# Strassen's scheme for the output products of the state-space part and of the last feed-forward

## Chip, cores, metric

The kernel runs on one core of a Trainium2 chip. The metric is the device time of one execution in microseconds (us); for the kernel before it is 3130.28 us, the median of three runs (3128.58 to 3131.64).

## What is computed

Two residual networks, one after the other, on 512 tokens of width 1024, all in float32. The first has a mixer of pooling and gated recurrence and a feed-forward part, then attention and a feed-forward part. The second, cut to what matters here, is

```python
for layer in range(DEPTH):                      # DEPTH = 2
    if layer < N_A_LAYERS:                      # layer 0: state space
        x = x + _mamba2_mixer(_rms_norm(x, a_norm[i]), ...)
    else:                                       # layer 1: attention with dilated windows
        ...
        x = x + _dilated_mixer(_rms_norm(x, b_norm[j]), k_sh, v_sh, ...)
    x = x + _conv_ffn(_rms_norm(x, ffn_norm[layer]), ...)
return _rms_norm(x, final_norm)
```

`_mamba2_mixer` ends in `y @ w_out` with y of 512 x 2048 and w_out of 2048 x 1024. `_conv_ffn` ends in `(silu(gate) * val) @ w_down` with a left side of 512 x 2816 and w_down of 2816 x 1024. The change is about the first of these and about the `w_down` of layer 1, which is the last product of the kernel.

## The kernel before, in words

Every large product is made three times as precise as one pass of TensorE in its float32r format gives: each operand is split into a high part h (a ScalarE copy into float32r, L312 or L321) and the rest l (a VectorE subtraction, L314 or L322), and `mm3` (L327 to L331) adds three matmuls, h*h, h*l and l*h, into one PSUM bank. Weights come in pieces of 128 x 1024 floats (512 KB) through `load_w`: SyncE's DMA into the tile wr (3 buffers), ScalarE's wh and VectorE's wl (4 buffers each).

`out_phase` makes an output product. The left side G (Y in the state-space part, GF in the feed-forward part) lies with its contraction index over the partitions, as nk pieces of 128 x 512 tokens. For each half hf of the 1024 output columns it takes four banks, one for each tile t of 128 tokens, and goes through the nk pieces: a `Jit` object splits G[:, k] just then into jh and jl, and four `mm3` calls of 128x512 follow. For the last six pieces of the second half it goes by tiles, so that tile after tile is finished and can be used early. A finished bank is handed to `use`: `residual_add` (L1202) adds it to x on VectorE; in the last feed-forward part `final_use` (L1632) also squares, scales and stores it.

What runs beside it: in `mamba` eight groups of heads (`ssd_group`) each make four heads' outputs, whose end is a chain over VectorE, ScalarE, GpSimd and TensorE (y, its squares, gms, the transposes yt, Y at L1414). `out_phase` needs Y piece by piece, so its first products stand in TensorE's queue among those of the last group. After it, `fill` makes the next part's normalized input: x is scaled (xn, L355), transposed (tr) and split; an `anchor` among the last products sets from where on TensorE takes these transposes. The order on every queue is made by a scheduler when the program is built; `high_priority(60)` lets the weights' loads and splits go ahead. Tiles come from pools; a tile whose memory still has a user waits for that user alone.

Of the kernel before, what the change touches and what calls it, by code (L numbers as in the profile page):

```python
# [9 lines left out]
FT = mybir.dt.float32  # L10
FR = mybir.dt.float32r
# [3 lines left out]
AF = mybir.ActivationFunctionType  # L15
# [4 lines left out]
P = 128  # L20
# [3 lines left out]
SEQ = 512  # L24
CTX = 256
TOK = SEQ + CTX
HID = 22
# [9 lines left out]
class Params:  # L37
# [5 lines left out]
    def add(self, name, width):  # L43
        self.off[name] = (self.n, width)
        self.n += width
# [161 lines left out]
class Jit:  # L207
# [5 lines left out]
    def pair(self, n):  # L213
        return [self.pool.tile([P, n], FR, name="j" + x, tag="j" + x, bufs=self.bufs) for x in "hl"]
# [30 lines left out]
class Body:  # L245
# [157 lines left out]
    def fill(self, norm, more=()):  # L403

        xt = self.xt
        part = lambda a: self.to_channels(
            self.scr, [self.x[:, t] for t in (a, a + 1)], self.p(norm), None, *xt[0], a * P,
            [(self.p(nm), *xt[1 + i]) for i, nm in enumerate(more)])
        with self.tc.issue_after(self.anchor):
            part(0)  # L410
        self.leave(lambda: part(2))
# [129 lines left out]
    def out_phase(self, pair, wap, nk, tiles, use, tail=3, order=None, first=0):  # L541

        for hf in range(2):
            acc = {t: self.bank("acc") for t in tiles}
            k0s = list(range(first, nk, 2))
            cut = len(k0s) - tail if hf else len(k0s)
            for k0 in k0s[:cut]:
                wh, wl = self.load_w(wap[:, hf, k0:k0 + 2])  # L550
                for k in range(k0, k0 + 2):
                    gh, gl = pair(k)
                    for t in tiles:
                        s = slice(t * P, (t + 1) * P)
                        self.mm3(acc[t], gh[:, s], gl[:, s], wh[:, k - k0], wl[:, k - k0], k == first, k == nk - 1)
            if cut == len(k0s):
                for t in tiles:
                    use(hf, t, acc[t])
                continue
            w = [(k0, self.load_w(wap[:, hf, k0:k0 + 2])) for k0 in k0s[cut:]]  # L560
            ks = [k0 + i for k0 in k0s[cut:] for i in (0, 1)]
            g = {k: pair(k) for k in ks} if not hasattr(pair, "tile") else None
            for t in order or tiles:
                s = slice(t * P, (t + 1) * P)
                gt = pair.tile(ks, t) if g is None else None
                for k0, (wh, wl) in w:
                    for i in (0, 1):
                        k = k0 + i
                        gh, gl = (g[k][0][:, s], g[k][1][:, s]) if g else (gt[0][:, k - ks[0]], gt[1][:, k - ks[0]])
                        self.mm3(acc[t], gh, gl, wh[:, i], wl[:, i], k == first, k == nk - 1)  # L570
                        if k == ks[1]:

                            self.anchor = self.last_mm
                use(hf, t, acc[t])

    def residual_norm(self, pool, x_of, row_of, tiles):

        nc = self.nc
        st = {}

        def use(hf, t, b):
            row = row_of(t)
            y = pool.tile([P, 512], FT, name=f"y{hf}", tag=f"y{hf}", bufs=2 if hf else tiles)
            if hf == 0:
                ms = pool.tile([P, 3], FT, name="yms", tag="yms", bufs=6)
                st[t] = (y, ms)
            y0, ms = st[t]
            self.squares(pool, b, ms[:, hf:hf + 1])
            nc.vector.tensor_mul(y, b, row[:, hf * 512:(hf + 1) * 512])
            if hf == 0:  # L590
                return
            r = ms[:, 2:3]
            nc.gpsimd.tensor_add(r, ms[:, 0:1], ms[:, 1:2])
            self.rstd(r, 1)
            x = x_of(t)
            for i, src in ((0, y0), (1, y)):
                s = slice(i * 512, (i + 1) * 512)
                nc.vector.scalar_tensor_tensor(x[:, s], src, r, x[:, s], op0=OP.mult, op1=OP.add)

        return use  # L600
# [598 lines left out]
        self.split(QH[:, hs, q], QL[:, hs, q], ob.rearrange("p (h q) -> p h q", h=4))  # L1199


    def residual_add(self, hf, t, b):  # L1202
        x = self.x[:, t, hf * 512:(hf + 1) * 512]
        self.nc.vector.tensor_add(x, x, b)
# [13 lines left out]
    def mamba(self, alloc, fill):  # L1218
        nc = self.nc
        es = ExitStack()  # L1220
        yp = self.pool("ssmy", es=es)
        Y = yp.tile([P, 16, SEQ], FT, name="Y")
        with ExitStack() as es1:
# [22 lines left out]
            b = self.bank("dt")[:32]  # L1246
            for k in range(KT):
                self.mm3(b, dh[:, k], dl[:, k], XH[:, k], XL[:, k], k == 0, k == KT - 1)
            with ExitStack() as es2:
                tp = self.pool("soft2", es=es2)  # L1250
                t = lambda n: tp.tile([32, SEQ], FT, name=n)
                v, u, z, w, acc = t("spv"), t("spu"), t("spz"), t("spw"), t("spa")
# [14 lines left out]
                b = self.bank("dtt")  # L1267
# [7 lines left out]
            b = self.bank("cs")  # L1275
# [19 lines left out]
        self.prepare(alloc)  # L1295
        with ExitStack() as es2:
            op = self.pool("ssmo", es=es2)
            self.out_phase(Jit(self, op, Y, SEQ, 3), self.a["wm_out"], 16, range(4), self.residual_add)
        fill()
        es.close()  # L1300

# [114 lines left out]
    def conv_ffn(self, l, side, alloc=None, fill=None):  # L1416
        nc = self.nc
        es = ExitStack()
        (XH, XL), = self.xt
        GF = self.pool(f"ug{l}", es=es, side=side).tile([P, HID, SEQ], FT, name="GF")  # L1420
        es2 = ExitStack()
        op = self.pool(f"uo{l}", es=es2, side=side)
        taps = self.p(f"fcw{l}").rearrange("p (a b) -> p a b", b=3)
        st = {}
        with ExitStack() as es1:
            tp = self.pool(f"ut{l}", es=es1, side=side)

            def use(j, i, b):
                k, val = j // 2, j % 2
                t = tp.tile([P, SEQ], FT, name="cv", tag=f"cv{val}", bufs=2)  # L1430
                self.conv(t, b, taps[:, HID * val + k], 3)
                if not val:
                    nc.scalar.activation(t, t, AF.Silu)
                    st[0] = t
                else:
                    nc.vector.tensor_mul(GF[:, k], t, st[0])

            self.in_phase(XH, XL, self.a[f"u{l}_in"], range(2 * HID), ((0, SEQ),), use, 3, HALVES)
        self.nes.close()
        if alloc:  # L1440
            self.prepare(alloc)
        self.out_phase(Jit(self, op, GF, SEQ, 3), self.a[f"u{l}_out"], HID, range(4),
                       self.residual_add if alloc else self.final_use(es2, side))
        es2.close()
        if fill:
            fill()
        es.close()
# [252 lines left out]
```

## Time and profile before

| what | us |
|---|---|
| median of three runs | 3130.28 |
| the profiled execution, its own time | 3131.54 |
| its span, first to last instruction | 3129.8 |
| TensorE (PE) busy, 15850 matmuls | 3055.1 |
| VectorE (DVE) busy | 1903.4 |
| ScalarE (ACT) busy | 1294.4 |
| GpSimd (POOL) busy | 138.1 |

The profile is of one execution; 1.7 us of its time lie outside the span. Times of the trace count from the span's start. Matmul records overlap, since the engine is a pipeline: the distance from start to start tells what one costs. The brackets behind a row give the idle time before it and what ended it. The granted clock of TensorE is full in nearly all of the span (0.997 on average).

### The profile page before, as it was taken

Reading aid. Unit: us, or ns where it says so; the run is one execution under the profiler, and the core shown is the slowest. Engines: PE = TensorE matmul, PEld = TensorE weight load, DVE = VectorE, ACT = ScalarE, POOL = GpSimd, SP = SyncE. Lnnn points to the kernel's source line nnn. Section 1 sums busy time; section 2 is a strip of 40 time slices with the busy share of each in tenths; the row PEclk is TensorE's granted clock in tenths of the full one; section 3 lists DMA queues with packets and bytes.
Section 4 is the critical chain, followed back from the end, with each engine's and each line's share of the span. In section 5 each row is a group of like instructions: output and inputs, shape, how many; then the busy total and the mean of one; then the engine's idle time right before and its main releaser. Section 6 shows DMA issues by size and latency. Waiting matters only on the chain. (4 is left out here: it accounts for less than half of the span.)

```text
span 3129.8 us, 40785 instructions
## 1 busy us (share of the span) xinstructions
PE 3055.1 (98%) x15850; PEld 2567.9 (82%) x15850; DVE 1903.4 (61%) x3252; ACT 1294.4 (41%) x2354; POOL 138.1 (4%) x244
## 2 busy tenths in 40 slices
PE   7999999999998999999999999999999999999999
PEld 6888788888886777888888888788888987788887
DVE  7996677532346677233567777665555687765555
ACT  4333451111335666222455455443334444543334
POOL 1000010000003101000010000000000000000000
PEclk9999999999999999999999999999999999999999
DMA  6621236632221111333322222233333321123332
GB/s 228 186 80 41 95 111 205 204 118 64 74 68 43 55 48 53 103 95 101 95 64 81 68 81 68 81 95 95 97 99 88 104 81 55 54 85 98 95 106 76
DMA packets 80929, 292.31 MB, mean 93 GB/s; under 512 B 9744, under 2 KB 10432, under 8 KB 79840
## 3 DMA queue, kind: packets, MB, share of 16 engines
q1 hardware_dynamic: 79104, 285.48, 30.2%
q0 software_dynamic: 1056, 3.17, 0.3%
q8 instruction: 125, 2.05, 0.3%
q10 hardware_dynamic: 576, 1.05, 0.1%
q14 instruction: 68, 0.56, 0.1%
HBM read 287.54 MB, written 2.12 MB: 93 GB/s over the span
## 5 line engine op out<-in xcount | busy, mean ns | idle before, releaser
L314 DVE TENSOR_TENSOR wl<-wr,wh 128x1024 fp32r<-128x1024 f32 x420 | 513.3, 1224 | 460.2 <-ACT wh L312 456.3
L312 ACT ACTIVATE wh<-wr 128x1024 fp32r<-128x1024 f32 x424 | 447.8, 1057 | 769.6 <-PE in L330 530.4
L329 PE MATMUL acc<-wh,jh 128*128 128x512 f32 x1080 | 424.4, 393 | 7.1 <-ACT jh L321 4.9
L331 PE MATMUL acc<-wh,jl 128*128 128x512 f32 x1080 | 422.0, 393 | 3.4 <-DVE jl L322 3.4
L330 PE MATMUL acc<-wl,jh 128*128 128x512 f32 x1080 | 423.5, 392 | 0.0
L322 DVE TENSOR_TENSOR jl<-GF,jh 128x512 fp32r<-128x512 f32 (+1 forms) x170 | 132.5, 781 | 233.9 <-ACT jh L321 230.2
L329 PEld LDWEIGHTS acc<-wh,jh 128*128 128x128 f32 x1080 | 203.2, 188 | 50.6 <-ACT jh L321 6.6
L321 ACT ACTIVATE jh<-GF 128x512 fp32r<-128x512 f32 (+1 forms) x170 | 119.0, 701 | 300.4 <-PE acc L330 288.8
L330 PE MATMUL in<-xtf0L,wh 128*128 128x256 f32 (+1 forms) x728 | 241.9, 332 | 0.0
L329 PE MATMUL in<-xtf0H,wh 128*128 128x256 f32 (+1 forms) x728 | 241.6, 332 | 0.0
L331 PEld LDWEIGHTS acc<-wh,jl 128*128 128x128 f32 x1080 | 202.9, 188 | 46.8 <-DVE jl L322 5.9
L331 PE MATMUL in<-xtf0H,wl 128*128 128x256 f32 (+1 forms) x728 | 241.2, 331 | 0.0
L330 PEld LDWEIGHTS acc<-wl,jh 128*128 128x128 f32 x1080 | 203.3, 188 | 40.6
L452 DVE SCALAR_TENSOR_TENSOR junkv<-wr,srow 128x1024 bf16<-128x1024 f32 x128 | 156.5, 1222 | 66.3 <-DMA wr<-ada 63.8
L329 PEld LDWEIGHTS in<-xtf0H,wh 128*128 128x128 f32 x728 | 138.3, 190 | 13.6
L331 PEld LDWEIGHTS in<-xtf0H,wl 128*128 128x128 f32 x728 | 138.1, 190 | 13.2
L330 PEld LDWEIGHTS in<-xtf0L,wh 128*128 128x128 f32 x728 | 138.3, 190 | 12.7
L330 PE MATMUL in<-xtf10L,wh 128*128 128x512 f32 (+1 forms) x376 | 141.2, 377 | 0.7 <-DVE xtf10L L322 0.4
L330 PE MATMUL in<-xtv0L,wh 128*128 128x512 f32 (+1 forms) x376 | 141.3, 376 | 0.0
L331 PE MATMUL in<-xtv0H,wl 128*128 128x512 f32 (+1 forms) x376 | 141.3, 376 | 0.0
L331 PE MATMUL in<-xtu0H,wl 128*128 128x512 f32 (+1 forms) x376 | 141.3, 376 | 0.0
L330 PE MATMUL in<-xtu0L,wh 128*128 128x512 f32 (+1 forms) x376 | 141.2, 376 | 0.0
(449 smaller groups left out, 6673.9 us busy)
## 6 DMA issues: line engine op xcount, KB each, us to landing
wr<-f_in SPq DMA_DIRECT2D x88, 512.0 KB, 3.6
wr<-u_in SPq DMA_DIRECT2D x88, 512.0 KB, 3.6
wr<-ada SPq DMA_DIRECT2D x80, 512.0 KB, 4.4
wr<-f_out SPq DMA_DIRECT2D x44, 512.0 KB, 3.6
wr<-u_out SPq DMA_DIRECT2D x44, 512.0 KB, 3.6
wr<-w_in SPq DMA_DIRECT2D x32, 512.0 KB, 3.8
wr<-wm_x SPq DMA_DIRECT2D x32, 512.0 KB, 3.6
wr<-wd_q SPq DMA_DIRECT2D x24, 512.0 KB, 3.5
```

Of the source, the lines that this page charges most:

```text
L312: nc.scalar.activation(h, raw, AF.Copy)
L314: (engine or nc.vector).tensor_sub(l, raw, h.bitcast(FT))
L321: nc.scalar.activation(h, src, AF.Copy)
L322: nc.vector.tensor_sub(l, src, h.bitcast(FT))
L329: mm(out, wh, xh, start=first, stop=False)
L330: mm(out, wh, xl, start=False, stop=False)
L331: self.last_mm = mm(out, wl, xh, start=False, stop=last).ins
L452: nc.vector.scalar_tensor_tensor(self.junkv, raw, 1.0, self.srow[:, v], op0=OP.mult, op1=OP.mult, accum_out=self.mc[l, v][:, j:j + 1])
```

## The change

Both output products are made by a new method `seven`, with Strassen's scheme in the form of Winograd. The tokens are halved (t0 and t1, 256 each), the contraction index is halved (k and half + k) and the output columns are halved (the two 512-wide parts of wap). Of the eight half-size products seven are left, of sums of the blocks. A first loop over half = nk/2 pieces makes four of them (m1, m6, m5, m4, eight banks in all) and a second loop the other three (m2, m3, m7). The sums of G's blocks are VectorE's (one of them GpSimd's in the second loop), the sums of the weights' blocks are GpSimd's: three of 128x512 in each step of the first loop, one in each of the second. The results of the first loop are joined on ScalarE and VectorE (c1, c2, c3) and added to x by GpSimd in the second loop (`residual_part`), two of 128x512 in each of four steps. Each weight is loaded once in the first loop, and three of four blocks again in the second. The other feed-forward part and the other products stay as they are. The last feed-forward part's pool for all this is opened later than the one before.

```diff
...
+    def seven(self, pool, G, wap, nk, use, add):
...
+        def raw(src, own):
+            r = (pool if own else self.wp).tile([P, 2, 512], FT, name="wr", tag="wr", bufs=2 if own else 3)
+            nc.sync.dma_start(r if len(src.shape) == 3 else r[:, 0], src)
+            return r
+        def right(r):
+            h, l = [self.wp.tile([P, 2, 512], FR, name="w" + x, tag="w" + x, bufs=4) for x in "hl"]
+            self.split(h, l, r)
+            return h, l
+        def left():
+            return [pool.tile([P, 4, H], FR, name="s" + x, tag="s" + x, bufs=3) for x in "hl"]
+        def sums():
+            return pool.tile([P, 2, H], FT, name="ss", tag="ss", bufs=2)
+        def product(m, k, hl, i, wh, wl, ts=(0, 1)):
+            for t in ts:
+                s = slice(t * P, (t + 1) * P)
+                self.mm3(m[t], hl[0][:, i, s], hl[1][:, i, s], wh, wl, k == 0, k == half - 1)
+        m1, m6 = [[self.bank("acc") for _ in range(2)] for _ in range(2)]
+        m5, m4 = [[self.bank("m") for _ in range(2)] for _ in range(2)]
+        part = {}
+        for k in range(half):
+            with self.tc.high_priority(60):
+                a, b = raw(wap[:, :, k], False), raw(wap[:, :, half + k], True)
+                g.tensor_sub(a[:, 1], a[:, 1], a[:, 0])
+                g.tensor_sub(b[:, 1], b[:, 1], a[:, 1])
+                g.tensor_sub(b[:, 0], b[:, 1], b[:, 0])
+                (ah, al), (bh, bl) = right(a), right(b)
+            s, hl = sums(), left()
+            dve.tensor_add(s[:, 0], G[:, k, t1], G[:, half + k, t1])
+            dve.tensor_sub(s[:, 1], s[:, 0], G[:, k, t0])
...
+            self.split(hl[0][:, :2], hl[1][:, :2], ends)
+            self.split(hl[0][:, 2:], hl[1][:, 2:], s)
+            nc.scalar.activation(G[:, half + k, t1], s[:, 1], AF.Copy)
+            last = k == half - 1
+            product(m1, k, hl, 0, ah[:, 0], al[:, 0])
...
+            product(m6, k, hl, 3, bh[:, 1], bl[:, 1])
+            if last:
+                for i in range(2):
+                    part[0, 2 + i] = pool.tile([P, 512], FT, name=f"c3{i}")
+                    dve.tensor_add(part[0, 2 + i], m6[i], part[0, i])
+            product(m5, k, hl, 2, ah[:, 1], al[:, 1])
+            if last:
+                for i in range(2):
+                    part[1, i] = part[1, 2 + i] = pool.tile([P, 512], FT, name=f"c2{i}")
+                    dve.tensor_add(part[1, i], m5[i], part[0, 2 + i])
+            product(m4, k, hl, 1, bh[:, 0], bl[:, 0])
+            if last:
+                for i in range(2):
+                    dve.tensor_sub(part[0, 2 + i], part[0, 2 + i], m4[i])
+        m2, m3 = [[self.bank("acc") for _ in range(2)] for _ in range(2)]
+        m7 = [self.bank("m") for _ in range(2)]
+        kept = []
+        todo = [(hf, t) for t in range(4) for hf in range(2)]
+        for k in range(half):
+            with self.tc.high_priority(60):
+                b, a = raw(wap[:, :, half + k], True), raw(wap[:, 1, k], False)
+                g.tensor_sub(a[:, 0], b[:, 1], a[:, 0])
+                bh, bl = right(b)
+                th, tl = [pool.tile([P, 512], FR, name="t" + x, tag="t" + x, bufs=3) for x in "hl"]
+                self.split(th, tl, a[:, 0])
+            s, hl = sums(), left()
+            dve.tensor_sub(s[:, 0], G[:, half + k, t0], G[:, half + k, t1])
+            g.tensor_sub(s[:, 1], G[:, k, t0], G[:, k, t1])
+            self.split(hl[0][:, 0], hl[1][:, 0], G[:, half + k, t0])
+            self.split(hl[0][:, 1:3], hl[1][:, 1:3], s)
+            if k:
+                for hf, t in todo[:2]:
+                    add(hf, t, part[hf, t])
+                todo = todo[2:]
+            last = k == half - 1
+            for i in range(2):
+                product(m2, k, hl, 0, bh[:, 0], bl[:, 0], (i,))
+                product(m3, k, hl, 1, bh[:, 1], bl[:, 1], (i,))
+                if last:
+                    use(0, i, m2[i])
+                    use(1, i, m3[i])
+            if k < half - 2:
+                product(m7, k, hl, 2, th, tl)
+            else:
+                kept.append((k, hl, 2, th, tl))
+        for i in range(2):
+            for args in kept:
+                product(m7, *args, (i,))
+            if i == 0:
+                self.anchor = self.last_mm
+            for hf in range(2):
+                use(hf, 2 + i, m7[i])
...
+    def residual_part(self, hf, t, part):
+        x = self.x[:, t, hf * 512:(hf + 1) * 512]
+        self.nc.gpsimd.tensor_add(x, x, part)
...
         with ExitStack() as es2:
             op = self.pool("ssmo", es=es2)
-            self.out_phase(Jit(self, op, Y, SEQ, 3), self.a["wm_out"], 16, range(4), self.residual_add)
+            self.seven(op, Y, self.a["wm_out"], 16, self.residual_add, self.residual_part)
         fill()
         es.close()
@@ -1419,7 +1537,8 @@
         (XH, XL), = self.xt
         GF = self.pool(f"ug{l}", es=es, side=side).tile([P, HID, SEQ], FT, name="GF")
         es2 = ExitStack()
-        op = self.pool(f"uo{l}", es=es2, side=side)
+        if alloc:
+            op = self.pool(f"uo{l}", es=es2, side=side)
...
         self.nes.close()
         if alloc:
             self.prepare(alloc)
-        self.out_phase(Jit(self, op, GF, SEQ, 3), self.a[f"u{l}_out"], HID, range(4),
-                       self.residual_add if alloc else self.final_use(es2, side))
+            self.out_phase(Jit(self, op, GF, SEQ, 3), self.a[f"u{l}_out"], HID, range(4), self.residual_add)
+        else:
+            op = self.pool(f"uo{l}", es=es2, side=side)
+            self.seven(op, GF, self.a[f"u{l}_out"], HID, self.final_use(es2, side), self.residual_part)
         es2.close()
         if fill:
             fill()
```

On TensorE's queue at the end of the state-space part (yd, yo and yt belong to the last group of heads, the acc of L329 to L331 to the output product) stood before:

```order
L1399 MATMUL yo<-H,Cc 128x256
L331 MATMUL acc<-wh,jl 128x512
L329 MATMUL acc<-wh,jh 128x512
L330 MATMUL acc<-wl,jh 128x512
L331 MATMUL acc<-wh,jl 128x512
L1390 MATMUL yd<-xdt,M_16273 128x128 x3
L1390 MATMUL yd<-xdt,M_16243 128x128
L1390 MATMUL yd<-xdt,M_16253 128x128
L1390 MATMUL yd<-xdt,M_16263 128x128
L1390 MATMUL yd<-xdt,M_16273 128x128
L1399 MATMUL yo<-H,Cc 128x256
L329 MATMUL acc<-wh,jh 128x512
```

and now stands, up to the first products of the new method:

```order
L1517 MATMUL yo<-H,Cc 128x256
L1508 MATMUL yd<-xdt,M_16273 128x128 x3
L1508 MATMUL yd<-xdt,M_16243 128x128
L1508 MATMUL yd<-xdt,M_16253 128x128
L1508 MATMUL yd<-xdt,M_16263 128x128
L1508 MATMUL yd<-xdt,M_16273 128x128
L1517 MATMUL yo<-H,Cc 128x256
L1530 MATMUL yt<-ident,y 128x128 x8
L329 MATMUL acc<-wh,sh 128x512
L330 MATMUL acc<-wl,sh 128x512
```

Before, 61 matmuls of the output product stood ahead of the group's last transpose; now none does.

On GpSimd's queue there was nothing between the last group's gms and the ms of the next part:

```order
L342 TENSOR_SCALAR gms_15861<-gms_15861 128x4
L343 TENSOR_TENSOR gms_15861<-gms_15861,mhalf_77 128x4
L342 TENSOR_SCALAR gms_16275<-gms_16275 128x4
L343 TENSOR_TENSOR gms_16275<-gms_16275,mhalf_77 128x4
L342 TENSOR_SCALAR ms_16974<-ms_16974 128x1
```

In the first loop it now has, for one piece after another (the first tile of a pair of wr is a, the second b):

```order
L617 TENSOR_TENSOR wr_16514<-wr_16514,wr_16512 128x512
L618 TENSOR_TENSOR wr_16514<-wr_16514 128x512
L616 TENSOR_TENSOR wr_16610<-wr_16610 128x512
L617 TENSOR_TENSOR wr_16563<-wr_16563,wr_16561 128x512
L618 TENSOR_TENSOR wr_16563<-wr_16563 128x512
```

and VectorE in the same steps:

```order
L322 TENSOR_TENSOR wl_16569<-wr_16561,wh_16568 128x1024
L322 TENSOR_TENSOR sl_16627<-Y_12795,sh_16626 128x512
L322 TENSOR_TENSOR wl_16573<-wr_16563,wh_16572 128x1024
L322 TENSOR_TENSOR sl_16627<-ss_16625,sh_16626 128x512
L621 TENSOR_TENSOR ss_16723<-Y_12795 128x256
L622 TENSOR_TENSOR ss_16723<-ss_16723,Y_12795 128x256
```

The subtraction of a (L616) goes two pieces ahead of those of b (L617, L618), and VectorE's six operations of a step are two splits of weights, two of the left side and two sums.

## Rows read from the trace of the kernel before

**Rows 1.** The page, part 1: busy us (share of the span) and instructions.

```profile
PE 3055.1 (98%) x15850; PEld 2567.9 (82%) x15850; DVE 1903.4 (61%) x3252; ACT 1294.4 (41%) x2354; POOL 138.1 (4%) x244
```

**Rows 2.** Timeline of PE at the last product: start, us, what [idle before].

```profile
3117.66 0.39 PE L329 MATMUL acc<-wh,jh 128*128 128x512 f32 x1
...
3122.20 0.39 PE L331 MATMUL acc<-wh,jl 128*128 128x512 f32 x1
```

**Rows 3.** Timeline of POOL, then of DVE, 12 to 53 us.

```profile
12.80 2.35 POOL L314 TENSOR_TENSOR wl<-wr,wh 128x1024 fp32r<-128x1024 f32 x1
...
36.51 5.92 POOL L314 TENSOR_TENSOR wl<-wr,wh 128x1024 fp32r<-128x1024 f32 x2 [9.46 <-ACT wh L312]
45.47 2.98 POOL L314 TENSOR_TENSOR wl<-wr,wh 128x1024 fp32r<-128x1024 f32 x1 [3.04 <-ACT wh L312]
...
36.16 0.69 DVE L322 TENSOR_TENSOR XL<-mod,XH 128x512 fp32r<-128x512 f32 x1
36.77 3.43 DVE L671 SCALAR_TENSOR_TENSOR junkv<-wo,srow 128x1024 bf16<-128x1024 f32 x1
...
46.18 2.55 DVE L322 TENSOR_TENSOR XL<-mod,XH 128x256 fp32r<-128x256 f32 x1
...
51.55 0.41 DVE L322 TENSOR_TENSOR XL<-mod,XH 128x256 fp32r<-128x256 f32 x1
51.88 1.21 DVE L671 SCALAR_TENSOR_TENSOR junkv<-wo,srow 128x1024 bf16<-128x1024 f32 x1
```

**Rows 4.** Timeline of POOL, then of DVE, 991 to 997 us.

```profile
995.99 0.74 POOL L378 TENSOR_TENSOR x1L<-mod,x1H 128x256 fp32r<-128x256 f32 x1 [2.12 <-ACT x1H L377]
...
991.38 0.42 DVE L322 TENSOR_TENSOR x1L<-mod,x1H 128x256 fp32r<-128x256 f32 x1
...
996.25 0.75 DVE L322 TENSOR_TENSOR x1L<-mod,x1H 128x256 fp32r<-128x256 f32 x1 [0.69 <-ACT x1H L321]
```

**Rows 5.** Last group and first output products: timeline of DVE and ACT, group of PE.

```profile
1955.73 1.23 DVE L314 TENSOR_TENSOR wl<-wr,wh 128x1024 fp32r<-128x1024 f32 x1 [6.99 <-ACT wh L312]
1956.87 0.68 DVE L1344 TENSOR_TENSOR xdt<-xt,dtT 128x512 f32<-128x512 f32 x1
...
1972.64 0.69 DVE L1382 TENSOR_TENSOR M<-sg,cbm 128x512 f32<-128x512 f32 x1 [0.27 <-ACT sg L1380]
...
1978.97 0.69 DVE L322 TENSOR_TENSOR jl<-Y,jh 128x512 fp32r<-128x512 f32 x1
...
1985.30 1.27 ACT L1414 ACTIVATE Y<-yt,prm 128x512 f32<-128x512 f32 x2
...
L329 PE MATMUL acc<-wh,jh x28: 387/389/582, 1964.3 to 1989.8; 128*128 128x512 f32 x28
```

**Rows 6.** Groups by line, ACT: busy us, mean ns of one, idle before.

```profile
L312 ACT ACTIVATE wh<-wr 128x1024 fp32r<-128x1024 f32 x424 | 447.8, 1057 | 769.6 <-PE in L330 530.4 <-DMA wr<-f_in 115.0 <-PE acc L331 52.0
...
L321 ACT ACTIVATE jh<-GF 128x512 fp32r<-128x512 f32 (+1 forms) x170 | 119.0, 701 | 300.4 <-PE acc L330 288.8 <-DVE GF L1436 11.6
```

**Rows 7.** Stretches: length, busy us of PE, PEld, DVE, ACT, POOL, clock, DMA, GB/s.

```profile
2064.00:2068.00 4.00, 4.00 (x35) 4.00 (x34) 1.92 (x3) 1.15 (x2) 0.73 (x2) 1.00 0.97 362
```

**Rows 8.** End of the first output product: group of PE, timeline of DVE.

```profile
L331 PE MATMUL acc<-wh,jl x101: 389/389/477, 1990.2 to 2060.2; 128*128 128x512 f32 x101
...
2053.37 0.75 DVE L355 TENSOR_SCALAR xn<-x,ms 128x1024 f32<-128x1024 f32 x1 [2.19 <-POOL ms L343]
```

**Rows 9.** Timeline at the start of the last product: PE, DVE.

```profile
3002.55 0.39 PE L329 MATMUL acc<-wh,jh 128*128 128x512 f32 x1
...
3006.32 0.69 DVE L1436 TENSOR_TENSOR GF<-cv 128x512 f32<-128x512 f32 x1
```

**Rows 10.** Timeline of PE after a long wait.

```profile
48.78 0.79 PE L331 MATMUL acc<-wh,XL 128*128 128x512 f32 x1 [5.37 <-DVE XL L322]
49.38 0.63 PE L329 MATMUL acc<-wh,XH 128*128 128x512 f32 x1
49.80 0.63 PE L330 MATMUL acc<-wl,XH 128*128 128x512 f32 x1
```

More of the change, by code (lines that the diff above doesn't have):

```diff
@@ L574, in out_phase @@
                 use(hf, t, acc[t])
+    def seven(self, pool, G, wap, nk, use, add):
+        nc, half, H = self.nc, nk // 2, 2 * P
+        t0, t1 = slice(0, H), slice(H, 2 * H)
+        T = G.shape[2]
+        dve, g = nc.vector, nc.gpsimd
+        def raw(src, own):
[27 more added lines that the diff above has]
+            dve.tensor_sub(s[:, 1], s[:, 0], G[:, k, t0])
+            base = G[:, k, 0:1]
+            ends = bass.AP(tensor=base.tensor, offset=base.offset,
+                           ap=[list(base.ap[0]), [half * T + H, 2], [1, H]])
+            self.split(hl[0][:, :2], hl[1][:, :2], ends)
[5 more added lines that the diff above has]
+                for i in range(2):
+                    part[0, i] = pool.tile([P, 512], FT, name=f"c1{i}")
+                    nc.scalar.activation(part[0, i], m1[i], AF.Copy)
+            product(m6, k, hl, 3, bh[:, 1], bl[:, 1])
[36 more added lines that the diff above has]
+                product(m3, k, hl, 1, bh[:, 1], bl[:, 1], (i,))
+                if last:
+                    use(0, i, m2[i])
[4 more added lines that the diff above has]
+                kept.append((k, hl, 2, th, tl))
+        for i in range(2):
+            for args in kept:
[4 more added lines that the diff above has]
+                use(hf, 2 + i, m7[i])
```

## Prediction

> **What bounds the kernel now.** I read the page first: TensorE is busy for 3055.1 of 3129.8 us [rows 1], so a shorter product pays only where TensorE then has no new wait. Next the timeline of TensorE near the end gives the price of one product: 21 matmuls of 128x512 follow each other from 3117.66 to 3122.20, 4.54/20 = 0.227 us from start to start, though a record lasts 0.39 [rows 2]. They overlap, so 0.39 must not be multiplied. Last I read VectorE and GpSimd (DVE and POOL in the rows) where both are busy at once, because the change puts GpSimd beside VectorE in both stages. The reader is to see there that the two take turns.
>
> **What is removed.** The two products had 16 x 4 x 2 x 3 = 384 and 22 x 4 x 2 x 3 = 528 matmuls. Now each k of the first loop has 4 products x 2 tiles x 3 = 24 and each of the second 18: 8 x 42 = 336 and 11 x 42 = 462. 114 fewer at 0.227 are **25.9 us** if nothing else changes. A step of the first loop then takes TensorE 24 x 0.227 = 5.45 us, of the second 4.09.
>
> **What GpSimd and VectorE pay: turns.** A GpSimd subtraction of 128x1024 takes 2.35 us when left alone. At 36.51 two of them take 5.92, and the VectorE operation issued at 36.77, of a kind that lasts 1.21 at 51.88, takes 3.43. At 46.18 a VectorE subtraction that lasts 0.41 elsewhere takes 2.55, beside a GpSimd one from 45.47 [rows 3]. Worked out: VectorE's previous operation ends at 36.85 and the GpSimd pair at 42.43; with one VectorE operation of 1.14 between, each GpSimd one holds (42.43 - 36.85 - 1.14)/2 = 2.22 us, in which VectorE stands still, and VectorE's own hold GpSimd back. At 128x256, VectorE's 0.42 becomes 0.75 beside a GpSimd subtraction from 995.99 [rows 4]: that one holds until 996.25 + 0.33, 0.59 us. For 128x512, a third of the way, I take 0.59 + 1.63/3 = **1.13 us**. VectorE's share is from start to start: 1.14 us at 1024 elements (1955.73 to 1956.87) [rows 5], 0.61 at 512 (36.16 to 36.77), 0.33 at 256 (51.55 to 51.88) [rows 3].
>
> The Trainium skill says the same in other measure (SBUF — State Buffer, Who interferes with whom): a VectorE instruction with two SBUF inputs and a GpSimd one that reads SBUF lock each other out, the first one for its whole instruction. The trace agrees on the lock [rows 3], not on "whole": the next VectorE start comes 0.08 us before the record before ends. With whole records the sum below would be 35 us longer; that is a rival with a chance of its own.
>
> Every VectorE split and sum of the new method reads two SBUF tiles, and so do all its GpSimd operations. So one step costs, in turns:
> - first loop: VectorE 2 x 1.14 + 2 x 0.61 + 2 x 0.33 = 4.16, GpSimd 3 x 1.13 = 3.39; **7.55 us against TensorE's 5.45**;
> - second loop: VectorE 1.14 + 2 x 0.61 + 2 x 0.33 = 3.02, GpSimd 1.13 + 0.59 = 1.72; **4.74 against 4.09**, and once per stage eight additions to x on GpSimd, 8 x 1.13 = 9.0.
>
> GpSimd alone (3.39) or VectorE alone (4.16) would hide behind TensorE; their sum does not. ScalarE does not bind: 2 x 1.06 + 2 x 0.70 and a copy of half that width are 3.9 us a step [rows 6]. Nor does the DMA: by their shapes the loops read 14.7 and 20.2 MB where 8.4 and 11.5 were read, at most 1.05 MB in a step, 139 GB/s at 7.55 us, where one stretch moved 362 [rows 7]. Buffers don't bind either: two of b allow a step each 7.55 us if load, two subtractions, copy and split fit into 15.
>
> **State-space stage.** Before, the last group's chain ran from 1955.7 to its Y at 1985.30 + 1.27 = 1986.6, and TensorE began the output products at 1964 beside it [rows 5]; the order shows 61 of them ahead of the last transpose, 13.8 us. Now all stand behind it. The chain gets shorter, since 3 splits of 1.14 and 6 of 0.61 leave VectorE, which waited but once there (0.27): 7.1 us. Two early GpSimd subtractions come in, 2.3. So Y ends at 1981.8 and the first split of Y at 1982.4 (if VectorE does not set the chain, up to 5 us later). By then these turns are paid: three first subtractions, one weight split, four sums, four subtractions for b, 10.4. The work in turns is 8 x 7.55 = 60.4 and 8 x 4.74 + 9.0 = 46.9. The last split releases 24 matmuls, 5.4. TensorE ends at 1982.4 + 50.0 + 46.9 + 5.4 = 2084.7; before it was 2060.2 + 0.4 = 2060.6 [rows 8]. That is **+24.1**. Hand-over to the next stage: tile 1 was normalized at 2053.37, 7 us before the last product [rows 8]; now its last addition waits for the second-last pair of products, with 12 matmuls (2.7 us) as cover for about 4 us of adding, squaring and scaling, and then the transposes. Bounds 0 to 6, I take **+4**.
>
> **Last feed-forward.** The new pool lies on memory that the input product still reads, so its sums and b loads wait for that product's end (3002.5) and VectorE's turn comes after its last GF at 3006.32 + 0.69 = 3007.0 [rows 9]. Before, TensorE went on without a gap. Work in turns: 11 x 7.55 = 83.1, less 4.5 done ahead (three subtractions, one split), and 11 x 4.74 + 9.0 = 61.1. TensorE ends at 3007.0 + 78.6 + 61.1 + 5.4 = 3152.1 against 3122.20 + 0.4 [rows 2]: **+29.5**. At the very end both halves of tile 3 now come together: another addition and multiplication (0.69 each), a scaling and a share of the wait for GpSimd, **+2.5** (0 to 4).
>
> **Sum.** 24.1 + 4 + 29.5 + 2.5 = +60.1. The saved 25.9 is already in it: the turns replace TensorE's time. The profiled execution took 3131.54 us, so 3191.6; the median lies 1.3 lower, so **3190 us**.
>
> **The range.** Below: if each VectorE operation holds only 0.08 less (the overlap of the records), a step loses 0.48 and 0.40, 16.7 us over 19 steps of each loop, and with both end terms at 0, 3167. Above: whole records, 8.52 and 5.47 a step and 1.28 for an addition, +34.7: 3225. After a wait of TensorE its matmuls can also be slower: after one of 5.37 us they last 0.63 and lie 0.42 apart [rows 10] instead of 0.39 and 0.227, and at that rate 24 would bind at 10 us; a stretch or two of this add 5. So **3164 to 3230**.
>
> **The rivals.**
> - Whole records as turns (the page's rule): 3225. For it: the 256-wide case can't tell 0.08 us. Against: the start-to-start times [rows 3]. Chance 0.12.
> - No turns in the steady loop, on the other side. Its mechanism: GpSimd gets ahead and its subtractions fall into VectorE's waits for ScalarE, so each loop runs at TensorE's 5.45 and 4.09. It decides below 5.45 us of turns a step, where I have 7.55. Then the first stage starts at 1982.4, waits 3 us for b's first weights (ScalarE has six splits, two copies and these, 5.8 us, while TensorE has 12 matmuls, 2.7) and needs 336 x 0.227: 2061.7 + 0.4, +1.5, and +4. The last one starts two sums and a split after 3007.0, at 3008.2; with 1 us for b and 462 x 0.227 it ends at 3114.5, -8, and +2.5. Together 0: **3130**. Against it: in each collision [rows 3, 4] one of the two stands still, and per step both have work for more than half of 5.45 us. Chance 0.08; of it 0.02 faster, 0.05 the same, 0.01 slower.
> - The change does all that it says and both starts are covered: 3130 - 26 = **3104**. Against it: the order at the last group. Chance 0.05.
>
> The forecast has the other 0.75. 0.2%, 6 us, is about what a measurement of this kernel can tell from no change. Faster 0.02 + 0.05 = 0.07, same 0.05, slower 0.75 + 0.12 + 0.01 = 0.88. The range holds most of the first two cases, 0.8.
>
> **What would show it.** In the new profile L616, L617 and L618 last longer than 1.28 us, about 1.13 plus the VectorE operation that they wait for; wl and sl records of VectorE in the two stages lie far above 1.23 and 0.69; TensorE is busy about 7 tenths in the first loops, waiting for VectorE and ScalarE; the loops last near 60 and 47 us, and 83 and 61. TensorE without such waits in the first loops and GpSimd at 1.28 us would prove me wrong; TensorE waiting for DMA would prove the wrong resource; an end of the first stage's Y later than 1984 would fault the chain.

## The result, and the profile after

The changed kernel takes **3206.5 us** (median of 3204.83 to 3207.91) where the kernel before, run beside it, takes 3129.9: ratio 1.0244, interval 1.0227 to 1.0262. The forecast was 3190, in a range of 3164 to 3230. The profiled execution took 3207.03, its span is 3205.2, so 75.4 longer than the span before.

The page, part 1, of the changed kernel:

```profile
PE 3064.1 (96%) x15736; PEld 2563.5 (80%) x15736; DVE 2030.1 (63%) x3363; ACT 1326.9 (41%) x2419; POOL 315.9 (10%) x355
```

Against [rows 1], TensorE has 114 matmuls fewer, as worked out, and yet 9 us more of busy time: some of them ran slower. GpSimd has gained 178 us of busy time and VectorE 127. Where that lies is told by stretches of the two loops of the state-space part and of the two loops of the last feed-forward part (length; busy us of PE, PEld, DVE, ACT, POOL; granted clock; DMA):

```profile
1994.00:2040.00 46.00, 38.29 (x153) 29.92 (x152) 39.17 (x37) 21.18 (x32) 32.00 (x20) 0.93 0.48 139
2044.00:2080.00 36.00, 29.79 (x102) 22.43 (x102) 32.19 (x34) 15.30 (x26) 29.17 (x19) 0.81 0.43 127
3052.00:3128.00 76.00, 63.18 (x250) 49.72 (x251) 72.19 (x59) 36.29 (x54) 52.03 (x33) 0.93 0.50 143
3135.00:3180.00 45.00, 36.34 (x140) 28.36 (x140) 41.10 (x41) 20.83 (x35) 33.54 (x23) 0.89 0.43 125
```

In each, VectorE is the busiest engine, TensorE waits, and GpSimd is busy more than two thirds of the time with work that needs far less when left alone. The groups of GpSimd's operations (busy us, mean ns of one) and the timeline of GpSimd, VectorE and TensorE in the first loop show why:

```profile
L617 POOL TENSOR_TENSOR wr<-wr 128x512 f32<-128x512 f32 x19 | 36.7, 1932 | 42.4 <-DMA wr<-u_out 24.7 <-DMA wr<-wm_out 9.9 <-DVE ss L621 5.2
L657 POOL TENSOR_TENSOR wr<-wr 128x512 f32<-128x512 f32 x19 | 35.5, 1871 | 12.2 <-DMA wr<-u_out 7.4 <-DMA wr<-wm_out 4.8
L618 POOL TENSOR_TENSOR wr<-wr 128x512 f32<-128x512 f32 x19 | 31.8, 1674 | 1.5
```

```profile
1998.45 1.27 POOL L616 TENSOR_TENSOR wr<-wr 128x512 f32<-128x512 f32 x1
...
2005.88 2.27 POOL L617 TENSOR_TENSOR wr<-wr 128x512 f32<-128x512 f32 x1
2008.23 1.62 POOL L618 TENSOR_TENSOR wr<-wr 128x512 f32<-128x512 f32 x1
2009.82 1.48 POOL L616 TENSOR_TENSOR wr<-wr 128x512 f32<-128x512 f32 x1
...
2006.93 1.77 DVE L322 TENSOR_TENSOR sl<-ss,sh 128x512 fp32r<-128x512 f32 x1
2008.62 2.95 DVE L621 TENSOR_TENSOR ss<-Y 128x256 f32<-128x256 f32 x2
2011.50 2.88 DVE L622 TENSOR_TENSOR ss<-ss,Y 128x256 f32<-128x256 f32 x2
2014.31 1.21 DVE L322 TENSOR_TENSOR wl<-wr,wh 128x1024 fp32r<-128x1024 f32 x1
...
2011.05 0.39 PE L329 MATMUL acc<-wh,sh 128*128 128x512 f32 x1
2015.57 0.80 PE L330 MATMUL acc<-wl,sh 128*128 128x512 f32 x1 [4.14 <-DVE wl L322]
```

A subtraction of GpSimd that takes 1.27 us alone takes 1.48 to 2.27 beside VectorE, and the pair of 128x256 sums, which VectorE does in 0.75 when alone, takes 2.95 and 2.88. The weight split that TensorE needs stands in VectorE's queue behind these sums, so TensorE stands still for 4.14 us. It is the collision of [rows 3], now in most steps. After such a wait the matmuls last 0.63 instead of 0.39 us, as in [rows 10]: the clocks of 0.81 to 0.93 above are means over time at 2.4 and at 1.2 GHz.

The limits of the stages come from the groups of the first and the last products, and of the last feed-forward part's:

```profile
L329 PE MATMUL acc<-wh,sh x64: 387/389/797, 1982.6 to 2086.3; 128*128 128x512 f32 x64
...
L331 PE MATMUL m<-th,sl x16: 388/389/628, 2050.0 to 2089.5; 128*128 128x512 f32 x16
...
L329 PE MATMUL acc<-wh,sh x88: 388/389/797, 3041.4 to 3187.3; 128*128 128x512 f32 x88
...
L331 PE MATMUL m<-th,sl x22: 388/389/398, 3135.5 to 3190.5; 128*128 128x512 f32 x22
```

The state-space product ends at 2089.9 (2060.6 before, +29.3). The last product begins at 3041.4 (3002.55 before [rows 9], +38.9) and ends at 3190.9 (3122.6, +68.3). The span's last 7.1 us of difference lie behind it.

### The profile page after: what moved, and what is told of

Read it like the earlier page. It is cut to its first block, busy times and chain, and to the rows that moved or that the text cites. A ratio compares the mean times of both kernels' runs of the same rounds, so it can differ in the third digit from the quotient of the medians.

```text
span 3205.2 us, 41001 instructions
## 1 busy us (share of the span) xinstructions
PE 3064.1 (96%) x15736; PEld 2563.5 (80%) x15736; DVE 2030.1 (63%) x3363; ACT 1326.9 (41%) x2419; POOL 315.9 (10%) x355
## 5 line engine op out<-in xcount | busy, mean ns | idle before, releaser
L314 DVE TENSOR_TENSOR wl<-wr,wh 128x1024 fp32r<-128x1024 f32 x382 | 466.5, 1223 | 442.9 <-ACT wh L312 439.0
L312 ACT ACTIVATE wh<-wr 128x1024 fp32r<-128x1024 f32 x386 | 407.9, 1058 | 762.7 <-PE in L330 546.3
L329 PE MATMUL acc<-wh,jh 128*128 128x512 f32 x776 | 305.6, 394 | 7.2 <-ACT jh L321 4.9
L331 PE MATMUL acc<-wh,jl 128*128 128x512 f32 x776 | 304.4, 394 | 3.4 <-DVE jl L322 3.4
L330 PE MATMUL acc<-wl,jh 128*128 128x512 f32 x776 | 305.6, 394 | 0.0
L329 PE MATMUL in<-xtf0H,wh 128*128 128x256 f32 (+1 forms) x728 | 241.6, 332 | 0.0
L331 PE MATMUL in<-xtf0H,wl 128*128 128x256 f32 (+1 forms) x728 | 241.1, 331 | 0.0
L322 DVE TENSOR_TENSOR jl<-GF,jh 128x512 fp32r<-128x512 f32 (+1 forms) x128 | 102.3, 801 | 189.6 <-ACT jh L321 186.5
L321 ACT ACTIVATE jh<-GF 128x512 fp32r<-128x512 f32 (+1 forms) x128 | 91.6, 718 | 234.4 <-PE acc L330 228.6
L329 PEld LDWEIGHTS acc<-wh,jh 128*128 128x128 f32 x776 | 146.3, 189 | 39.0 <-ACT jh L321 6.6
L331 PEld LDWEIGHTS acc<-wh,jl 128*128 128x128 f32 x776 | 146.3, 189 | 34.6 <-DVE jl L322 5.5
L330 PEld LDWEIGHTS acc<-wl,jh 128*128 128x128 f32 x776 | 146.3, 189 | 29.3
L329 PEld LDWEIGHTS in<-xtf0H,wh 128*128 128x128 f32 x728 | 138.3, 190 | 13.5
L331 PEld LDWEIGHTS in<-xtf0H,wl 128*128 128x128 f32 x728 | 138.2, 190 | 13.2
L330 PEld LDWEIGHTS in<-xtf0L,wh 128*128 128x128 f32 x728 | 138.3, 190 | 12.8
L331 PE MATMUL in<-xtv0H,wl 128*128 128x512 f32 (+1 forms) x376 | 141.3, 376 | 0.0
L331 PE MATMUL in<-xtu0H,wl 128*128 128x512 f32 (+1 forms) x376 | 141.3, 376 | 0.0
```

The costliest lines, as they stand in the source:

```text
L312: nc.scalar.activation(h, raw, AF.Copy)
L314: (engine or nc.vector).tensor_sub(l, raw, h.bitcast(FT))
L321: nc.scalar.activation(h, src, AF.Copy)
L322: nc.vector.tensor_sub(l, src, h.bitcast(FT))
L329: mm(out, wh, xh, start=first, stop=False)
L330: mm(out, wh, xl, start=False, stop=False)
```

## The experiments

The kernel before ran beside each of them, between 3129.8 and 3130.1 us. Only times are used here: no run measures how precise the split products are.

**1 and 2. Each place alone.** The first kernel puts the old call back in the last feed-forward part (and opens its pool where it was), the second does so in the state-space part:

```diff
-            self.seven(op, GF, self.a[f"u{l}_out"], HID, self.final_use(es2, side), self.residual_part)
+        self.out_phase(Jit(self, op, GF, SEQ, 3), self.a[f"u{l}_out"], HID, range(4),
+                       self.residual_add if alloc else self.final_use(es2, side))
```

```diff
-            self.seven(op, Y, self.a["wm_out"], 16, self.residual_add, self.residual_part)
+            self.out_phase(Jit(self, op, Y, SEQ, 3), self.a["wm_out"], 16, range(4), self.residual_add)
```

> The new method in the state-space part alone; the last feed-forward part as before. By the two traces TensorE ends that product 29.3 us later (2089.9 against 2060.6) and begins the last one about 38 us later. If each place pays its own cost, this gives 3130 + 38 = 3168; if the 8 us between are not of this place (other tiles' places in memory, for instance) it gives 3159. By the terms of the prediction alone 24.1 + 4: 3158.

> The new method in the last feed-forward part alone; the state-space part as before. By the two traces this place adds 75.4 - 38 = 37 us: 3167. By the terms of the prediction alone 29.5 + 2.5: 3162. If the two places share a cost, the two single kernels add up to more or less than 76 us.

Measured: 3169.4 with the state-space part alone (ratio 1.0125, 1.0109 to 1.0142), 3168.2 with the last feed-forward part alone (1.0120, 1.0104 to 1.0136). The losses, 39.3 and 38.1, add up to 77.3 (before rounding) against 76.7 for both. So each place pays its own cost, and also the some 8 us between the two products in the trace belong to the first place.

**3. The sums on VectorE.**

```diff
-                g.tensor_sub(a[:, 1], a[:, 1], a[:, 0])
+                dve.tensor_sub(a[:, 1], a[:, 1], a[:, 0])
...
-        self.nc.gpsimd.tensor_add(x, x, part)
+        self.nc.vector.tensor_add(x, x, part)
```

> All sums that the new method gives to GpSimd (L616 to L618, L657, L663, L1318) go to VectorE instead; nothing else changes. Theory of turns: GpSimd's turn of 1.13 us for 512 elements becomes VectorE's 0.61. A step of the first loop costs 4.16 + 3 x 0.61 = 6.0 us instead of 7.55, of the second 4.09 (TensorE) instead of 4.74, and the eight additions 4.9 instead of 9.0 a stage: 19 x 1.55 + 19 x 0.65 + 2 x 4.1 = 50 us less, near 3156. Rival, the loops are paced by something else (a chain from load to product, ScalarE, the two buffers of b): VectorE, already the busier engine, only gets 1.83 us more a step: 3206 or up to 35 us slower, 3241.

Measured: 3171.9 (1.0130, 1.0114 to 1.0146), 34.7 less. Giving the busiest engine more work made the kernel faster, as turns would have it: VectorE does for 0.61 us what cost it 1.13 to stand by. A shorter way from load to product would point in the same direction, but the rival of experiment 4 prices that way at 24 us at most, even with the sums gone altogether. The gain is two thirds of the 50 expected. A stretch of the first and of the second loop of this kernel says why:

```profile
1990.00:2020.00 30.00, 29.12 (x120) 21.37 (x119) 29.70 (x44) 17.48 (x26) 0.00 (x0) 1.00 0.58 172
2036.00:2066.00 30.00, 28.37 (x114) 22.21 (x114) 29.44 (x52) 14.55 (x23) 0.00 (x0) 0.93 0.45 130
```

VectorE is full in both. My 4.09 us for the second loop was TensorE's. VectorE has there 8 x 3.96 us of splits and sums, 4.9 for the eight additions, and, which I had left out, 3.7 for the six joining operations c and 3.4 for three weight splits of the next part: 43.7 us, nearly the 46.9 of the turns before. The second loops gained only 0.9 and 4.0 us. The first loops gained what was expected: the one of the state-space part went from 61.2 (1982.6 to 2043.8) to 49.2 us, against 48 by the sum, the other from 89.6 to 72.4.

**4 and 5. The sums left out**, first the three of the first loop, then every GpSimd operation of the method:

```diff
-                g.tensor_sub(a[:, 1], a[:, 1], a[:, 0])
-                g.tensor_sub(b[:, 1], b[:, 1], a[:, 1])
-                g.tensor_sub(b[:, 0], b[:, 1], b[:, 0])
...
-                    add(hf, t, part[hf, t])
+                    pass
```

> Leaves out the three sums of weight blocks per step of the first loop (L616 to L618), so the products are made of the plain blocks; loads, splits and matmuls stay as many. Theory of turns: VectorE's 4.16 us a step falls under TensorE's 5.45, a step costs 5.45 instead of 7.55: 19 x 2.1 = 40 us less, near 3166. Rival, chain or buffers: the two sums of b lie in the chain from load to product, but with two of b in flight only half of their 2.5 us a step shows, and where ScalarE or the loads pace it nothing does: 3182 to 3206.

> Leaves out every GpSimd operation of the new method: the sums of weights in both loops, the sum of the left side on GpSimd, and the eight additions of finished parts to x. Matmuls, splits and loads stay. Theory: both loops are now TensorE's, the second ones 8 x 4.09 + 5.4 = 38 and 11 x 4.09 + 5.4 = 50 us instead of 44.9 and 57.1 as measured without the weight sums of the first loop alone: 13.5 less than that kernel's 3163, 3149.5. What is then left over 3104 is no turn: lost cover at both starts, the way to the next part, and the end. Rival, the second loops wait for something else (b's loads, ScalarE): near 3163.

Measured: 3163.0 (1.0104, 1.0086 to 1.0122) and 3135.5 (1.0019, 1.0010 to 1.0028). The first is 43.5 less than the changed kernel, where the turns of the first loops gave 40; the rival of a chain, 3182 or more, falls. The second is 27.6 less again; I had expected 13.5, because I counted the last 24 matmuls of each second loop (5.4 us) twice in TensorE's time; by the prediction's own terms it is 19 x 0.65 + 18.0 = 30.4. First the stretches of the kernel without the three sums (first loop, second loop), then of the kernel without any:

```profile
1990.00:2020.00 30.00, 30.00 (x134) 24.86 (x133) 23.92 (x35) 19.28 (x30) 3.94 (x3) 1.00 0.62 191
2030.00:2054.00 24.00, 15.54 (x53) 11.31 (x52) 20.33 (x18) 9.22 (x15) 21.50 (x14) 0.83 0.42 124
```

```profile
1990.00:2020.00 30.00, 30.00 (x134) 24.84 (x134) 26.46 (x40) 20.40 (x33) 0.00 (x0) 1.00 0.70 218
2030.00:2054.00 24.00, 24.00 (x108) 19.89 (x107) 19.80 (x37) 14.35 (x28) 0.00 (x0) 1.00 0.67 202
```

Where GpSimd is silent, TensorE is full at clock 1.00; where it works, TensorE waits and its clock falls to 0.83. Altogether GpSimd's operations cost 3206.5 - 3135.5 = **71 us**. The page of this kernel shows that VectorE had been standing by:

```profile
PE 3041.4 (97%) x15736; PEld 2556.8 (82%) x15736; DVE 1955.7 (62%) x3382; ACT 1328.8 (42%) x2438; POOL 139.0 (4%) x244
```

VectorE is busy 74 us less than in the changed kernel (2030.1), though it has 19 operations more (in each step of the second loop one split of the left side became two). And even without any GpSimd operation the scheme is not faster than the kernel before.

**6 and 7. One more GpSimd operation per step**, with two SBUF inputs and with one:

```diff
+                d = pool.tile([P, 512], FT, name="dd", tag="dd", bufs=1)
+                g.tensor_sub(d, a[:, 1], a[:, 0])
```

```diff
+                g.tensor_scalar(d, a[:, 0], 2.0, None, op0=OP.mult)
```

> One more GpSimd subtraction of 128x512 in each step of the first loops, of two blocks of a into a tile that nobody reads: the suspected cost once more. Theory of turns: 1.13 us of VectorE's time per step, 8 + 11 steps: 21.5 us more than the changed kernel, 3228. Rival, GpSimd has idle time (3.4 to 5 us of work in a step of 7.55) and hides it: 3206. If whole records were the turns, 1.28 a step: 3231, not to be told from the first.

> The same added operation, but with one SBUF input instead of two (a times 2, into a tile that nobody reads). If only GpSimd operations with two inputs take turns with VectorE, it falls into GpSimd's idle time: 3206. If any GpSimd operation that reads SBUF does, it costs up to as much as the other: 3206 to 3228, by how long it holds.

Measured: 3221.5 (1.0294, 1.0279 to 1.0309), 14.9 more; and 3211.3 (1.0259, 1.0243 to 1.0274), 4.8 more. The intervals of the second and of the changed kernel overlap; those of the two added operations do not.

Over 19 steps this would be 0.79 and 0.25 us a step, but in the traces the first loops pay more. In both kernels the method's first matmul comes at 1979.23 instead of 1982.63: the last group of heads begins 1.6 us earlier, and its matmuls are less slow (14 matmuls yd take 1.83 instead of 2.76 us). Why is open. First the ends of the first loops of the changed kernel (its starts are shown above), then starts and ends with the added subtraction:

```profile
L331 PE MATMUL m<-wh,sl x32: 388/389/628, 1986.2 to 2040.8; 128*128 128x512 f32 x32
L331 PE MATMUL m<-wh,sl x44: 388/389/628, 3047.5 to 3128.3; 128*128 128x512 f32 x44
```

```profile
L329 PE MATMUL acc<-wh,sh x64: 388/389/794, 1979.2 to 2093.0; 128*128 128x512 f32 x64
L331 PE MATMUL m<-wh,sl x32: 388/389/628, 1982.8 to 2045.4; 128*128 128x512 f32 x32
L329 PE MATMUL acc<-wh,sh x88: 387/389/628, 3047.7 to 3202.7; 128*128 128x512 f32 x88
L331 PE MATMUL m<-wh,sl x44: 387/389/794, 3055.9 to 3145.0; 128*128 128x512 f32 x44
```

From its first to its last matmul, one loop went from 58.2 to 66.2 us, the other from 86.9 to 97.3: 18.4 us or 0.97 a step, not far from the 1.13 of one turn. With the single input they last 64.2 and 90.6 us, 9.7 more or 0.51 a step. So a turn of GpSimd is hardly hidden in the first loops. No product waits for the added result, so it puts no further sum into the way from load to product; it only delays the next sums in GpSimd's queue, and the operation with one input does that for longer (1.66 against 1.35 us in the middle) and costs half. GpSimd and VectorE in that kernel's first loop:

```profile
2007.04 2.47 POOL L620 TENSOR_SCALAR dd<-wr 128x512 f32<-128x512 f32 x1
...
2006.93 1.23 DVE L322 TENSOR_TENSOR wl<-wr,wh 128x1024 fp32r<-128x1024 f32 x1 [2.28 <-ACT wh L321]
2008.08 1.10 DVE L322 TENSOR_TENSOR sl<-ss,sh 128x512 fp32r<-128x512 f32 x1
2009.10 0.75 DVE L623 TENSOR_TENSOR ss<-Y 128x256 f32<-128x256 f32 x2
```

Here it is GpSimd that is stretched (2.47 us, 1.49 at least), while the split of 1.23 and the two sums of 0.75 run as when alone; only the middle one loses 0.42.

**8. The lost cover by itself.** The kernel before, whose state-space product takes the four PSUM banks that the last group of heads uses:

```diff
-            acc = {t: self.bank("acc") for t in tiles}
+            acc = {t: self.bank(name) for t in tiles}
...
-            self.out_phase(Jit(self, op, Y, SEQ, 3), self.a["wm_out"], 16, range(4), self.residual_add)
+            self.out_phase(Jit(self, op, Y, SEQ, 3), self.a["wm_out"], 16, range(4), self.residual_add, name="m")
```

> The kernel before, with nothing changed but the four PSUM banks of the state-space part's output product: it takes those that the last group of heads still uses, as the new method must, since its four products need all eight. Theory: this alone takes the cover away; the product starts behind the last transposes, near 1980.5 as in the kernel without weight sums, and lasts 384 x 0.227 = 87.2 and some 2 us of slow start: 2069.7 against 2060.6, so 3139. Rival, the cover was worth nothing because the last group's chain gets shorter by what it loses: 3130. Against both, the full 61 products: 3144.

Measured: 3142.7 (1.0041, 1.0027 to 1.0055), 12.8 more. The bank choice alone puts the product behind the last transposes, in its first and last matmuls:

```profile
1981.56 1.97 PE L1412 MATMUL yt<-ident,y 128*128 128x128 f32 x8 [5.17 <-ACT y L1410]
1983.18 0.78 PE L329 MATMUL m<-wh,jh 128*128 128x512 f32 x1
...
L331 PE MATMUL m<-wh,jl x128: 388/390/629, 1984.2 to 2073.5; 128*128 128x512 f32 x128
```

It ends at 2073.9 instead of 2060.6: 13.3 us, nearly all of the 61 matmuls (13.8). I had expected 9, with a product that starts at 1980.5; it started at 1983.18, with matmuls of 0.63 us.

**9 and 10. The last three steps by tiles**, in the kernel without GpSimd's operations and in the whole one:

```diff
-            if k < half - 2:
+            if k < half - 3:
...
+        for i in range(2):
+            for k, hl, bh, bl, th, tl in kept:
+                product(m2, k, hl, 0, bh[:, 0], bl[:, 0], (i,))
+                product(m3, k, hl, 1, bh[:, 1], bl[:, 1], (i,))
+            use(0, i, m2[i])
+            use(1, i, m3[i])
```

> The kernel without any GpSimd operation of the new method (the same parts left out), with the last three steps of the second loop taken by tiles: for each of the first two tiles 18 matmuls of m2 and m3, then for each of the last two 9 of m7, instead of 12 of the last step and 12 of m7 for four tiles. The same matmuls, loads and splits. Theory: of the 31 us by which that kernel (3135.5) misses 3104, some 8 stand between the products and 7 at the end because the four tiles come within 5.4 us and VectorE and ScalarE finish them one after another; spread out as before (18 matmuls a tile), about 4 us come back at each place: 3127. Rival, the places cost what they do for another reason (slow matmuls after the gap, weights of the next part, the longer list of VectorE as such): 3133 to 3136.

> The changed kernel, complete, with the same last steps by tiles. Theory: here VectorE and GpSimd set the pace and TensorE waits; the last split now releases 54 matmuls (12.3 us) instead of 24 (5.4), so each stage ends up to 7 us later on TensorE, against about 4 us that come back behind it: 3206 to 3212. If the ends were all, it would gain as in the other kernel: 3198.

Measured: 3132.7 (1.0008, 0.9999 to 1.0018), 2.8 less than without, and 3204.7 (1.0238, 1.0221 to 1.0255), 1.8 less than the changed kernel. Both differences are within the intervals, so they are read from the traces. The end behind the last matmul shrank as expected, in both from 14.3 to 10.5 us (7.2 before the change). The way to the next part did not (the first cv starts at 2080.6 instead of 2080.8): in VectorE's queue tile 1's xn still stands behind the additions of tiles 2 and 3:

```profile
2056.68 1.28 DVE L1320 TENSOR_TENSOR x<-x,acc 128x512 f32<-128x512 f32 x2
2057.88 1.28 DVE L1320 TENSOR_TENSOR x<-x,m 128x512 f32<-128x512 f32 x2
...
2060.21 1.28 DVE L1320 TENSOR_TENSOR x<-x,m 128x512 f32<-128x512 f32 x2
2061.41 0.75 DVE L355 TENSOR_SCALAR xn<-x,ms 128x1024 f32<-128x1024 f32 x1
```

So half of this theory held. In the whole kernel, where the last split releases more, the two products end 2.4 and 1.3 us later, and the effects nearly cancel. No kernel here beats the one before, and the experiments point to none: without GpSimd's part it takes 3135.5, and that part is not optional.

## Why the prediction was right, and where it was off

**The bound.** Right. In turns, VectorE and GpSimd have more to do in a step than TensorE: with the sums left out the loops run at TensorE's pace, with the sums on VectorE at VectorE's, with one more subtraction they get slower. It holds for the first loops and for about the first half of the second ones, but not to the end: TensorE's last wait in the two products is at 2070.31 (3.14 us) and at 3157.46 (3.48 us), and from there, with GpSimd's additions done, it runs without a gap for 20 and 33 us.

The terms in which GpSimd's operations exceed TensorE's step are (7.55 - 5.45) x 19 + (4.74 - 4.09) x 19 + 18.0 = 70.3 us; left out, they gave back 71. That the two agree to a microsecond is partly luck. The sum has GpSimd hold VectorE for all of 92 x 1.13 + 19 x 0.59 = 115 us, and VectorE's busy time grew by 74 only. What stands in for the rest is VectorE's own waits (6.8 of 46 us in the first stretch above), slow matmuls, and a first matmul that without GpSimd's part comes 1.6 us earlier; none of them was measured by itself.

The rival of whole records counts 3.07 x 19 + 1.38 x 19 + 16 x 1.28 = 105 the same way and falls as a forecast (3225). The lock of the Trainium skill (SBUF — State Buffer, Who interferes with whom) is thus seen here. Whether its turns are a little shorter than the records, or some of them do not collide, these runs do not separate: the overlap of 0.08 us, my reason for the first, is there between VectorE's records without GpSimd too (51.55 + 0.41 against 51.88 in [rows 3]). The rival without turns was put at 3130; the kernel without them takes 3135.5, so it was priced nearly right, but that it would happen was not: turns do collide. And 3104 would have needed the covers too.

**The terms that were mis-sized.** By the traces, in us:

| term | forecast | measured | from |
|---|---|---|---|
| state-space product, end of TensorE | +24.1 | +29.3 | 2089.9 - 2060.6 |
| way to the next part | +4 | +6.4 | first cv, 2111.1 - 2075.4, less 29.3 |
| parts between (not explained) | 0 | +1.8 | rest to the last input product's end |
| last product, from there to its end | +29.5 | +30.8 | 3190.9 - 3122.6, less 37.5 |
| behind the last matmul | +2.5 | +7.1 | 75.4 - 68.3 |
| sum | +60.1 | +75.4 | |

*The two products.* The first matmul came when forecast (1982.63 against a first split at 1982.4), with some luck: in experiments 6 and 7 it comes 3.4 us earlier, behind the same group of heads. VectorE's last split for the first product, and its last GF before the second:

```profile
2082.24 0.68 DVE L322 TENSOR_TENSOR sl<-ss,sh 128x512 fp32r<-128x512 f32 x1
...
3042.47 0.69 DVE L1555 TENSOR_TENSOR GF<-cv 128x512 f32<-128x512 f32 x1
```

In the state-space part the turns end at 2082.9 where the sum had 2079.3 (1982.4 + 50.0 + 46.9), 3.6 later; TensorE needs 7.0 us more instead of 5.4. In the last product VectorE's last split ends at 3183.25, the turns take 140.1 us from 3043.16 against 139.7 by the sum, and TensorE needs 7.6 us more. So the step that failed here is "the last split releases 24 matmuls": 30 and 32 were still to come, since TensorE was behind by then. TensorE was busy 0.83 of the first loops, not 7 tenths; slow matmuls after its waits, which I had only in the range, are in that (granted clock 0.93). How much of the +5.2 they make up was not measured by itself, nor how much of the 3.6 is the six operations c (3.7 us), which the sum put at nothing. That the 61 matmuls lose their cover was read from the order. Its cause I did not name: the four products of the first loop fill all eight PSUM banks, and experiment 8 gives it 12.8 us.

*The way to the next part.* The step that failed is its bound, "0 to 6". The first cv, before and after the change:

```profile
L1211 ACT ACTIVATE cv<-in,prm x12: 667/672/672, 2075.4 to 2129.6; 128x512 f32<-128x512 f32 x12
```

```profile
L1329 ACT ACTIVATE cv<-in,prm x42: 668/668/673, 2111.1 to 2328.5; 128x512 f32<-128x512 f32 x42
```

and TensorE's first transposes behind the last product, from the timeline of the changed kernel:

```profile
2092.66 1.97 PE L363 MATMUL tr<-ident,xn 128*128 128x128 f32 x8 [2.78 <-DVE xn L355]
```

TensorE waits 2.78 us for xn. Then come the 16 transposes, which before stood among the last products and so were part of the 2060.6; eight took 1.04 us there, so 16 are some 2 us. And now they start slowly: eight take 1.97.

*The end.* The forecast let one more addition and multiplication wait; but all four tiles come within 5 us, and VectorE finishes them in one queue. Its last rows:

```profile
3197.47 0.48 DVE L1774 TENSOR_SCALAR fo<-fo,fr 128x512 f32<-128x512 f32 x1 [1.00 <-POOL fr L343]
3197.87 0.68 DVE L1768 TENSOR_TENSOR fo<-x,fg 128x512 f32<-128x512 f32 x1
3198.47 0.68 DVE L1322 TENSOR_TENSOR x<-x,m 128x512 f32<-128x512 f32 x1
```

The last half of x, whose products ended at 3190.9, is added at 3198.47, behind the scaling of tile 2. Experiment 9 took 3.8 us of this back by spreading the tiles.

**The DMA, ScalarE and the buffers** did not bind, as forecast: in the kernel without GpSimd's part the loops run at TensorE's pace with the same loads and buffers and nearly the same ScalarE work. One wait for a load shows in the changed kernel: GpSimd waits 8.76 us for b's third piece, until 1994.02, and behind it VectorE waits 3.64 and TensorE 1.37 and 0.76 us.

## What to carry to other kernels

Before work goes to an engine because it is idle, look in the trace for places where it runs beside the engine that it is to relieve: two engines that take turns are one engine, and the sum of their turns is what has to fit beside the matmuls. Cost a scheme with fewer products by all that it takes away. By the traces of the kernel without GpSimd's part, 31 us were lost against the 25.9 saved before a single sum was paid: 9.7 in the first product, which lost its cover to the live accumulators, 6.6 on the way to the next part (2 of them transposes that only moved), 7.2 in the last product, which starts behind VectorE's last GF and with slow matmuls (0.63 us), and 7.1 at the end, where results finish together; 0.4 lies between. And an order listing shows that a cover is lost, but the cause (here the banks) has to be found by itself.

## What was not expected of the hardware

VectorE does not stand still for GpSimd when one of its two inputs lies in PSUM. GpSimd adds parts to x, and VectorE joins c from a bank and SBUF beside it:

```profile
2045.17 2.96 POOL L1318 TENSOR_TENSOR x<-x,c 128x512 f32<-128x512 f32 x2
...
2045.68 1.28 DVE L639 TENSOR_TENSOR c<-acc,c 128x512 f32<-128x512 f32 x2
2046.88 1.27 DVE L644 TENSOR_TENSOR c<-m,c 128x512 f32<-128x512 f32 x2
```

Two take 1.28 us as anywhere, and GpSimd's two 1.48 each. The same section of the Trainium skill states this for a VectorE operation with at most one SBUF input that is not in one of its two-port modes, and the trace agrees. That a GpSimd operation with one input costs so much less than one with two (0.51 against 0.97 us a step of the first loops) was seen in experiment 7 alone.
